# Four of the eight output jobs of the last block move behind its projections, and a staging tile gets a second place

## The chip, the cores and the metric

The kernel runs on one core of a Trainium2 chip. The metric is the device time of one execution in microseconds (us); of a set of timed executions the median counts. Engines: PE (TensorE, matmuls), DVE (VectorE), ACT (ScalarE), POOL (GpSimd) and SP (SyncE, which issues nearly all DMAs here). Each engine runs its own instructions strictly in the order in which they were written for it, and waits on semaphores for the others.

## The reference, cut to what matters

Two residual layers on x of shape (1, 2048, 1024). Layer 0 is RWKV-7 time mixing beside a gated short convolution, layer 1 a Conformer convolution beside a Mamba-2 SSD. The change lies in layer 1:

```python
p = h @ od_w_in[j]                      # 2048 x 1024 times 1024 x 3080
y_c = conformer_conv_mix(p[..., :CF_COLS], cf_conv_w[j], cf_conv_b[j], cf_ln_g[j], cf_ln_b[j])
y_d = mamba2_ssd_mix(p[..., CF_COLS:], ...)
y = jnp.concatenate([y_c, y_d], axis=-1) @ od_w_out[j]     # 2048 x 1024 times 1024 x 1024
x = x + gate[:, None, :] * rms_norm(y, norm_post[i])

def conformer_conv_mix(p, conv_w, conv_b, ln_g, ln_b):
    val, glu_gate, g = jnp.split(p, 3, axis=-1)
    u = val * jax.nn.sigmoid(glu_gate)
    u = causal_dwconv(u, conv_w) + conv_b                  # 31 taps
    u = jax.nn.silu(layer_norm(u, ln_g, ln_b))             # over 512 channels
    return u * jax.nn.silu(g)
```

## The kernel before

The 2048 rows are worked in four blocks of 512 (`NB` = 4). A block of layer 1 is a list of 25 projection jobs (`odd`): `dt`, eight tiles for the SSD's x, B and C (`evac_xbc`), four SSD gates, then four groups of three for the Conformer (GLU gate, value, gate). A job is 24 matmuls of 128x512 (8 parts of the contraction, each in three products of split fp32) into one of three PSUM tiles `pp`; only `dt` has 16. After the value job of group g, `evac_val` writes `u`, and `conv31` runs 30 multiply-adds `co<-u,cfw,co` on DVE. When the last gate is out, `conf_out` (lines 1281 to 1325) transposes the four `co` tiles by PE, takes mean and variance (`bst`, `bmv`), normalises to `xn`, transposes back, and for each of the four groups writes a tile `cs` with ACT, multiplies twice on DVE, splits it (`yh` by ACT, the rest by DVE) and stores both to DRAM (`y<-yh`, `y<-cs`). `cs` comes from `take`, which waits, while the order is being written, until the former holder has been freed; it is freed when its store is issued.

An output job multiplies one tile of 128 rows of y with one half (`dh`) of the output weights. It loads its y by two DMAs `w<-y` of 512 KB; the weights of a half are loaded into one of two large tiles (`act0`, `act1`) by eight DMAs `act<-wo` of 512 KB. The other large tile holds the block's h. Each row tile has two output jobs. The first to run only keeps its product: ACT squares and copies it to `yo`, which goes to DRAM (`od<-yo`). The second finishes the tile: it loads the row tile `x` (512 KB, two places) and the kept half (`yo<-od`), then ACT squares, DVE adds up (`ss`), POOL takes the root, DVE does `pp<-pp,ss,gp`, `x<-x,pp` and `yo<-yo,ss,gp`, POOL adds `x<-x,yo`, and SP stores the row tile (`out<-x`).

Three things set the order. `tile_trunk` makes one list of jobs by hand: `put(block, at, what)` places something behind the projection number `at` of a block, and what is added to a block's list comes behind its last projection. `run_jobs` writes the jobs in that order, and after every fourth matmul (`pace`) `tick` lets one step of each queue of side work follow (convolution, SSD chunks, evacuations, stores). `Feed.fetch` loads the operands of up to two jobs ahead; for an output job it first waits until all eight y tiles of that block have had their stores issued (`when=ready(t)`). All row tiles of the last block are therefore out of reach until `conf_out` of that block is through.

In the last block eight output jobs stand among the projections: half 0 of row tiles 4 to 7 behind projections 3, 5, 7 and 9, half 1 of the same behind 12, 13, 15 and 16. Behind the last projection come half 1 and then half 0 of tiles 8 to 11, and then tiles 12 to 15 (the last block's own) in pairs of both halves, eight jobs. The weights are loaded three times: half 0, half 1, and half 0 again.

Of the kernel before, what the change touches and what calls it, by code (L numbers as in the profile page):

```python
# [18 lines left out]
P = 128  # L19
# [3 lines left out]
BL = 512  # L23
# [125 lines left out]
class Trunk:  # L149
# [1134 lines left out]
    def conf_out(self, b, st):  # L1284
        nc = self.nc
        V, A, G, TE = nc.vector, nc.scalar, nc.gpsimd, nc.tensor
        add, mult = ALU.add, ALU.mult
        t = self.t
        co, cg = st["co"], st["cg"]
        xn = []  # L1290
        yield from self.pause(8)
        for q in range(4):
            ps = yield from self.take("tr", [P, BL], 2)
            for g in range(4):
                TE.transpose(out=ps[:, g * P:(g + 1) * P], in_=co[g][:, q * P:(q + 1) * P], identity=self.ident)
            yield
            sts = self.small.tile([P, 6], F32, name="bst")
            V.bn_stats(out=sts, in_=ps)
            mv = self.small.tile([P, 2], F32, name="bmv")
            V.bn_aggr(out=mv, in_=sts)  # L1300
            G.tensor_scalar(out=mv[:, 1:2], in0=mv[:, 1:2], scalar1=1e-5, scalar2=None, op0=add)
            G.tensor_tensor(out=mv[:, 1:2], in0=mv[:, 1:2], in1=self.nhalf[:, 0:1], op=ALU.pow)
            yield from self.pause(3)
            x = t.tile([P, BL], F32, name="xn", bufs=4)
            V.tensor_scalar(out=x, in0=ps, scalar1=mv[:, 0:1], scalar2=mv[:, 1:2], op0=ALU.subtract, op1=mult)
            self.free(ps)
            xn.append(x)
            yield
        for g in range(4):
            ps = yield from self.take("tr", [P, BL], 2)  # L1310
            for q in range(4):
                TE.transpose(out=ps[:, q * P:(q + 1) * P], in_=xn[q][:, g * P:(g + 1) * P], identity=self.ident)
            yield
            w = yield from self.take("cs", [P, BL])
            A.activation(out=w, in_=ps, func=AF.Identity, scale=self.col("cf_g", g, g + 1), bias=self.col("cf_lb", g, g + 1))
            th = t.tile([P, BL], F32, name="pr", bufs=2)
            A.activation(out=th, in_=ps, func=AF.Tanh, scale=self.hcfg[:, g:g + 1], bias=self.hcflb[:, g:g + 1])
            self.free(ps)
            yield
            V.scalar_tensor_tensor(out=w, in0=th, scalar=1.0, in1=w, op0=add, op1=mult)  # L1320
            V.scalar_tensor_tensor(out=w, in0=w, scalar=0.25, in1=cg[g], op0=mult, op1=mult)
            self.free(cg[g])
            yield from self.y_store(1, b, g, w)
            yield
# [229 lines left out]
def tile_trunk(ctx, tc, I, out, T):  # L1554
    k = Trunk(ctx, tc, I, out, T)
    k.setup()
    NB = T // BL
    with ExitStack() as e:
        k.st = e.enter_context(tc.tile_pool(name="st0", bufs=1))
        k.t = e.enter_context(tc.tile_pool(name="t0", bufs=1))  # L1560
        k.even_setup()
        blocks = [k.even(b) for b in range(NB)]
        list(k.first_block([o[0] for o in blocks[0][:BEGUN]]))
        blocks[0] = blocks[0][BEGUN:]
        k.slow += [k.modulation(0, range(16, 24), 1), k.modulation(1, range(24), 1), k.gate_row(0)]
        keys = iter(range(4 * NB))

        def outs(l, ts, dh):
            key = "wo", next(keys)
            return (lambda: k.urgent.append(k.w_out(l, dh, key))), k.out_jobs(l, ts, dh, key)  # L1570

        ahead = lambda l, b, spread=1: [lambda: k.urgent.append(k.hblock(l, b, spread))]

        def put(block, at, what):

            n = [i for i, o in enumerate(block) if not callable(o) and o[2][0] != "wo"][at - 1] + 1 if at else 0
            while n < len(block) and (callable(block[n]) or block[n][2][0] == "wo"):
                n += 1
            block[n:n] = what

        split_wo = lambda l: [(I["w_out"][l, dh][:, k2 * D:(k2 + 1) * D], k.wo[l][dh][2 * k2:2 * k2 + 2]) for dh in range(2) for k2 in range(KT // 2)]
        split_w = [(I["w_in1"][j], k.w1[j]) for j in range(24)] + [(I["w_in1"][24], k.wdt)]
        put(blocks[1], 0, [lambda: k.slow.append(k.presplit(split_wo(0) + split_w + split_wo(1)))])
        for b in range(NB - 1):
            put(blocks[b], AHEAD0, ahead(0, b + 1))
        load, jobs = zip(*[outs(0, range(8), dh) for dh in range(2)])
        at = 1, 4, 5, 7, 8, 10, 11, 13, 14, 14, 19, 21, 23, 25
        for p, o in zip(at, [load[0], *jobs[0], load[1], *jobs[1][:4]]):
            put(blocks[-1], p, [o])
        put(blocks[-1], 32, ahead(1, 0, 2))  # L1590
        blocks[-1] += jobs[1][4:]
        order = sum(blocks, [])
        blocks = [k.odd(b) for b in range(NB)]
        tiles = lambda b: range(4 * b, 4 * b + 4)
        at = 1, 3, 5, 7, 9, 9, 12, 13, 15, 16
        for b, (l, ts) in enumerate([(0, tiles(2)), (0, tiles(3)), (1, tiles(0)), (1, tiles(1))]):
            last = b == NB - 1
            load, jobs = zip(*[outs(l, ts if not dh or not last else range(4, 4 * NB), dh) for dh in range(2)])
            for p, o in zip(at, [load[0], *jobs[0], load[1], *jobs[1][:4]]):
                put(blocks[b], p, [o])  # L1600
            if not last:
                put(blocks[b], at[-1], ahead(1, b + 1, 2))
            if b == 1:
                put(blocks[1], 23, [lambda: k.slow.append(k.gate_row(1))])
        again, first = outs(1, range(8, 4 * NB), 0)
        blocks[-1] += [again, *jobs[1][4:8], *first[:4]] + [j for two in zip(jobs[1][8:], first[4:]) for j in two]
        order1 = sum(blocks, [])
        feed = Feed(k, order + order1)
        k.run_jobs(order, feed)
        k.drain(k.ev, k.quick, k.aux, k.urgent, k.bg, k.post, k.tail)  # L1610
    with ExitStack() as e:
        k.st = e.enter_context(tc.tile_pool(name="st1", bufs=1))
        k.t = e.enter_context(tc.tile_pool(name="t1", bufs=1))
        k.odd_setup()
        k.gated, k.pace = False, PACE[1]
        k.run_jobs(order1, feed)
        k.drain(k.ev, k.quick, k.aux, k.bg, k.post, k.tail)
    return k
# [47 lines left out]
```

## Time and profile before

| | us |
|---|---|
| median of three runs | 2455.23 |
| lowest and highest | 2452.19, 2456.57 |
| the profiled execution | 2446.16 |
| its span, first to last instruction | 2444.4 |
| PE busy in it | 2208.9 (90%) |
| DVE busy in it | 1753.1 (72%) |
| mean granted TensorE clock | 0.947 of full speed |

The page gives each engine's share over the whole span; over 40 slices PE is busy nine tenths or more in most, and five and seven tenths in the last two. Where time can be won or lost is read from the stretch around the last block, from about 2095 us, by the time lines of PE, DVE, ACT and POOL, and from the chain of waits that ends last. In a time line a bracket at the end of a row gives the idle time of that engine ahead of it and what ended it.

### The profile page before, as it was taken

How to read it: one execution, taken by the hardware profiler on the slowest of the kernel's cores; microseconds unless marked ns; L12 is line 12 of the kernel's file. 1: busy time of each engine (PE TensorE's matmuls, PEld its weight loads, DVE VectorE, ACT ScalarE, POOL GpSimd, SP SyncE). 2: the span in 40 equal slices, each digit the busy share in tenths (PEclk: the TensorE clock that was granted, in tenths of full speed). 3: DMA queues.
4: the chain of work that ended last, by engine and by line, in shares of the span. 5: the costliest groups of instructions: out<-in, count | busy, mean ns of one | idle time of the engine just before them, and what ended most of it. 6: DMA issues, size and time to landing. Idle time of an engine off the chain costs nothing. (4 is left out here: it accounts for less than half of the span.)

```text
span 2444.4 us, 36532 instructions
## 1 busy us (share of the span) xinstructions
PE 2208.9 (90%) x13408; PEld 1728.7 (71%) x13408; DVE 1753.1 (72%) x3340; ACT 811.4 (33%) x1731; POOL 593.3 (24%) x792
## 2 busy tenths in 40 slices
PE   6688889898988989989999979999999999999957
PEld 4566667676766767667777667877778787878836
DVE  6797897867857778565377443689589859967961
ACT  4334223433233322221222432353443525252221
POOL 2544535335253140221042310210020012002021
PEclk9788989999898999999999989999999999999978
DMA  8675676776776544544788678867877786787756
GB/s 302 223 254 179 216 260 226 234 251 226 248 237 215 199 122 159 190 129 139 254 292 268 235 266 296 301 226 254 293 252 248 243 298 207 267 275 276 244 178 232
DMA packets 232390, 575.18 MB, mean 235 GB/s; under 512 B 20498, under 2 KB 70418, under 8 KB 232212
## 3 DMA queue, kind: packets, MB, share of 16 engines
q1 hardware_dynamic: 232068, 572.59, 69.2%
q8 instruction: 106, 1.74, 0.3%
q14 instruction: 72, 0.59, 0.1%
q10 hardware_dynamic: 144, 0.26, 0.0%
HBM read 436.91 MB, written 135.86 MB: 234 GB/s over the span
## 5 line engine op out<-in xcount | busy, mean ns | idle before, releaser
L111 PE MATMUL pp<-act,w 128*128 128x512 f32 x7000 | 1797.8, 408 | 47.0 <-DMA w<-y 22.0
L111 PEld LDWEIGHTS pp<-act,w 128*128 128x128 f32 x7000 | 1312.5, 193 | 343.5 <-DMA w<-y 22.4
L111 DVE SCALAR_TENSOR_TENSOR co<-u,cfw,co 128x512 f32<-128x512 f32 x480 | 345.3, 754 | 6.1 <-ACT co L111 5.8
L111 POOL TENSOR_SCALAR ss<-ss 128x1 f32<-128x1 f32 x80 | 27.0, 338 | 639.5 <-DVE ss L111 463.2
L111 POOL TENSOR_TENSOR x<-x 128x512 fp32r<-128x512 f32 x80 | 109.0, 1376 | 134.8 <-ACT x L111 134.2
L111 POOL TENSOR_SCALAR sp<-S,PL 128x64 f32<-128x64 f32 x128 | 66.2, 531 | 194.1 <-DVE S L111 193.8
L111 DVE TENSOR_TENSOR pr<-X,BK 128x2 f32<-128x2 f32 (+30 forms) x248 | 101.6, 410 | 6.2
L111 ACT ACTIVATE tA<-pp 128x512 f32<-128x512 f32 x64 | 38.1, 596 | 203.4 <-PE pp L111 201.5
L111 POOL TENSOR_TENSOR w<-x,w 128x512 fp32r<-128x512 f32 x57 | 83.6, 1479 | 56.6 <-ACT w L111 56.4
L111 DVE TENSOR_REDUCE X<-pr 128x1 f32<-128x2 f32 (+30 forms) x248 | 86.5, 349 | 6.1
L111 ACT ACTIVATE q<-pp,cp 128x512 f32<-128x512 f32 x65 | 44.7, 688 | 128.6 <-PE pp L111 106.8
L111 DVE TENSOR_TENSOR UV<-ch,scal 64x128 f32<-64x128 f32 x128 | 36.9, 289 | 58.3 <-PE ch L111 56.3
L111 POOL COPY q<-carry 128x1 f32<-128x1 f32 (+1 forms) x84 | 38.6, 460 | 155.0 <-DVE tG L111 65.0
L111 POOL COPY carry<-q 128x1 f32<-128x1 f32 (+1 forms) x84 | 22.3, 265 | 221.8 <-ACT q L111 172.3
L111 POOL TENSOR_TENSOR x<-x,yo 128x512 f32<-128x512 f32 x32 | 48.5, 1516 | 104.0 <-DVE yo L111 91.5
L111 DVE TENSOR_TENSOR ss<-oss 128x1 f32<-128x1 f32 x32 | 6.0, 189 | 92.1 <-ACT tA L111 92.0
L111 ACT CAST x<-x 128x512 fp32r<-128x512 f32 x80 | 46.6, 616 | 72.6 <-DMA w<-w 19.5
L111 DVE SCALAR_TENSOR_TENSOR tG<-pp,derived,q 128x512 f32<-128x512 f32 x65 | 48.4, 744 | 30.9 <-ACT q L111 30.5
L111 DVE TENSOR_TENSOR act<-tr,act 128x256 fp32r<-128x256 f32 (+1 forms) x120 | 51.3, 436 | 24.1 <-ACT act L111 23.4
L111 PE MATMUL tr<-cc,h 128*128 128x128 f32 x224 | 39.6, 293 | 31.8 <-ACT h L111 28.6
L111 DVE STREAM_TRANSPOSE BK<-SC 32x1024 f32<-32x1024 f32 x32 | 63.8, 1993 | 0.5
L111 ACT ACTIVATE yo<-pp 128x512 f32<-128x512 f32 x32 | 19.1, 597 | 127.9 <-PE pp L111 112.6
(273 smaller groups left out, 3164.6 us busy)
## 6 DMA issues: line engine op xcount, KB each, us to landing
w<-w SPq DMA_DIRECT2D x450, 512.0 KB, 4.3
w<-y SPq DMA_DIRECT2D x128, 512.0 KB, 4.4
act<-wo SPq DMA_DIRECT2D x88, 512.0 KB, 6.1
x<-in_w_in_dram SPq DMA_DIRECT2D x58, 512.0 KB, 5.5
w<-x SPq DMA_DIRECT2D x96, 256.0 KB, 3.4
h<-in_ada_w_dram SPq DMA_DIRECT2D x32, 512.0 KB, 4.9
y<-yh SPq DMA_DIRECT2D x64, 256.0 KB, 3.1
wo<-x SPq DMA_DIRECT2D x64, 256.0 KB, 3.5
```

What stands on the lines that cost most here:

```text
L111: return f(*args, **kw)
```

## The change

`cs` gets two places, so that group g+1 may be written while group g is still on its way to DRAM; this holds for all four blocks of layer 1. And the last block's order changes: only half 0 of row tiles 4 to 7 stands among the projections, behind 5, 10, 15 and 18. Behind the last projection stand half 0 of tiles 8 to 11, half 1 of tiles 4 to 11, and the eight jobs of tiles 12 to 15 in pairs: twelve jobs ahead of those eight, where there were eight. The weights are loaded twice, half 0 and then half 1.

```diff
-            w = yield from self.take("cs", [P, BL])
+            w = yield from self.take("cs", [P, BL], 2)
...
-        for b, (l, ts) in enumerate([(0, tiles(2)), (0, tiles(3)), (1, tiles(0)), (1, tiles(1))]):
-            last = b == NB - 1
-            load, jobs = zip(*[outs(l, ts if not dh or not last else range(4, 4 * NB), dh) for dh in range(2)])
-            for p, o in zip(at, [load[0], *jobs[0], load[1], *jobs[1][:4]]):
+        for b, (l, ts) in enumerate([(0, tiles(2)), (0, tiles(3)), (1, tiles(0))]):
+            load, jobs = zip(*[outs(l, ts, dh) for dh in range(2)])
+            for p, o in zip(at, [load[0], *jobs[0], load[1], *jobs[1]]):
                 put(blocks[b], p, [o])
...
-        again, first = outs(1, range(8, 4 * NB), 0)
-        blocks[-1] += [again, *jobs[1][4:8], *first[:4]] + [j for two in zip(jobs[1][8:], first[4:]) for j in two]
+        load, jobs = zip(*[outs(1, range(4, 4 * NB), dh) for dh in range(2)])
+        for p, o in zip((1, 5, 10, 15, 18), [load[0], *jobs[0][:4]]):
+            put(blocks[-1], p, [o])
+        blocks[-1] += [load[1], *jobs[0][4:8], *jobs[1][:8]] + [j for two in zip(jobs[0][8:], jobs[1][8:]) for j in two]
```

PE at the start of the last block, before: `pp_19145` is projection 3, `pp_19230` (on `act0`) the first output job, `pp_19288` projection 4. The matmuls of the two are interleaved where the output job's weights are still arriving.

```order
L111 MATMUL pp_19145<-act1_62,w_19066 128x512 x12
L111 MATMUL tr_19171<-cc_88,tA_19097 128x16 x4
L111 MATMUL pp_19145<-act1_62,w_19068 128x512 x12
L111 MATMUL pp_19230<-act0_61,w_19100 128x512 x12
L111 MATMUL pp_19230<-act0_61,w_19102 128x512 x6
L111 MATMUL pp_19288<-act1_62,w_19146 128x512 x7
L111 MATMUL pp_19230<-act0_61,w_19102 128x512 x3
L111 MATMUL pp_19288<-act1_62,w_19146 128x512 x4
L111 MATMUL pp_19230<-act0_61,w_19102 128x512 x3
L111 MATMUL pp_19288<-act1_62,w_19146 128x512
L111 MATMUL pp_19288<-act1_62,w_19148 128x512 x12
```

After: projections 4 (`pp_19230`) and 5 (`pp_19277`) follow at once, then an output job (`pp_19332`) and projection 6 (`pp_19395`).

```order
L111 MATMUL pp_19145<-act1_62,w_19066 128x512 x12
L111 MATMUL tr_19171<-cc_88,tA_19097 128x16 x4
L111 MATMUL pp_19145<-act1_62,w_19068 128x512 x12
L111 MATMUL pp_19230<-act1_62,w_19100 128x512 x12
L111 MATMUL pp_19230<-act1_62,w_19102 128x512 x12
L111 MATMUL pp_19277<-act1_62,w_19146 128x512 x12
L111 MATMUL pp_19277<-act1_62,w_19148 128x512 x12
L111 MATMUL pp_19332<-act0_61,w_19231 128x512 x12
L111 MATMUL pp_19332<-act0_61,w_19233 128x512 x12
L111 MATMUL pp_19395<-act1_62,w_19278 128x512 x12
```

So the first output job stands two projections later. Of the later ones, projection 15 (the first value job) has two output jobs ahead of it in the block in place of six.

PE at the end, before: the back transposes of the last two groups (`tr<-cc,xn`), and behind them the first job of tile 12, `pp_21343`.

```order
L111 MATMUL tr_21305<-cc_88,xn_21155 128x128
L111 MATMUL tr_21305<-cc_88,xn_21191 128x128
L111 MATMUL tr_21305<-cc_88,xn_21240 128x128
L111 MATMUL tr_21305<-cc_88,xn_21272 128x128
L111 MATMUL tr_21321<-cc_88,xn_21155 128x128
L111 MATMUL tr_21321<-cc_88,xn_21191 128x128
L111 MATMUL tr_21321<-cc_88,xn_21240 128x128
L111 MATMUL tr_21321<-cc_88,xn_21272 128x128
L111 MATMUL pp_21343<-act0_61,w_21339 128x512 x12
L111 MATMUL pp_21343<-act0_61,w_21341 128x512 x12
```

After: the last group's transposes (`tr_21232`) stand within the cover job `pp_21225`, a whole further one (`pp_21281`) follows, and then the first job of tile 12, `pp_21329`.

```order
L111 MATMUL pp_21225<-act1_62,w_21094 128x512 x4
L111 MATMUL tr_21232<-cc_88,xn_20942 128x128
L111 MATMUL tr_21232<-cc_88,xn_20994 128x128
L111 MATMUL tr_21232<-cc_88,xn_21045 128x128
L111 MATMUL tr_21232<-cc_88,xn_21081 128x128
L111 MATMUL pp_21225<-act1_62,w_21094 128x512 x8
L111 MATMUL pp_21225<-act1_62,w_21096 128x512 x12
L111 MATMUL pp_21281<-act1_62,w_21166 128x512 x12
L111 MATMUL pp_21281<-act1_62,w_21168 128x512 x12
L111 MATMUL pp_21329<-act0_61,w_21325 128x512 x12
```

All sixteen back transposes had no matmul between them; now they lie among the last four of the cover jobs that stand ahead of tile 12.

DVE at the same place, before: groups 2 and 3 of `cs`, and then the first finishing step of tile 12 (`ss_21428`).

```order
L111 SCALAR_TENSOR_TENSOR cs_21312<-pr_21314,cs_21312 128x512
L111 SCALAR_TENSOR_TENSOR cs_21312<-cs_21312,cg_20754 128x512
L111 TENSOR_TENSOR cs_21312<-cs_21312,yh_21318 128x512
L111 SCALAR_TENSOR_TENSOR cs_21328<-pr_21330,cs_21328 128x512
L111 SCALAR_TENSOR_TENSOR cs_21328<-cs_21328,cg_20879 128x512
L111 TENSOR_TENSOR cs_21328<-cs_21328,yh_21334 128x512
L111 TENSOR_TENSOR ss_21428<-oss_167 128x1
```

After: the last instruction on `cs_21245`, which the last store waits for, stands behind `ss_21321` and `pp_21281`, the finishing steps of the last cover job.

```order
L111 TENSOR_TENSOR x_21215<-x_21215,pp_21165 128x512
L111 SCALAR_TENSOR_TENSOR cs_21202<-cs_21202,cg_20566 128x512
L111 TENSOR_TENSOR cs_21202<-cs_21202,yh_21212 128x512
L111 SCALAR_TENSOR_TENSOR cs_21245<-pr_21247,cs_21245 128x512
L111 SCALAR_TENSOR_TENSOR yo_21274<-yo_21274,ss_21277,gp_17033 128x512
L111 SCALAR_TENSOR_TENSOR cs_21245<-cs_21245,cg_20700 128x512
L111 TENSOR_TENSOR ss_21321<-oss_167 128x1
L111 SCALAR_TENSOR_TENSOR pp_21281<-pp_21281,ss_21321,gp_17033 128x512
L111 TENSOR_TENSOR cs_21245<-cs_21245,yh_21255 128x512
L111 TENSOR_TENSOR x_21271<-x_21271,pp_21225 128x512
```

So finishing steps of cover jobs now lie between the steps of the last groups, and the last of them ahead of the last store.

## Rows read from the trace of the kernel before

**Rows 1.** Chain that ended last: start us, us, what.
```profile
2382.91 0.70 DVE cs L111
...
2383.62 2.47 DMA y<-cs
...
2386.37 3.66 DMA w<-y
...
2390.07 45.97 PE pp L111 x192
...
2436.07 0.60 ACT tA L111
...
2437.31 0.55 POOL ss L111
```

**Rows 2.** Time line of PE, 2300 to 2445 us: start, length, engine, operation, count, [idle].
```profile
2299.72 32.81 PE L111 MATMUL pp<-act,w 128*128 128x512 f32 x144
...
2344.26 0.44 PE L111 MATMUL tr<-cc,co 128*128 128x128 f32 x2 [2.38 <-DVE co L111]
...
2366.97 1.11 PE L111 MATMUL tr<-cc,xn 128*128 128x128 f32 x4 [6.33 <-ACT pr L111]
2390.07 45.96 PE L111 MATMUL pp<-act,w 128*128 128x512 f32 x192 [21.98 <-DMA w<-y]
```

**Rows 3.** Time line of DVE, 2105 to 2400 us, same columns.
```profile
2200.65 0.16 DVE L111 TENSOR_TENSOR ss<-oss 128x1 f32<-128x1 f32 x1 [9.07 <-ACT tA L111]
...
2220.14 0.69 DVE L111 SCALAR_TENSOR_TENSOR u<-tA,pp 128x512 f32<-128x512 f32 x1 [2.90 <-PE pp L111]
...
2231.95 0.76 DVE L111 SCALAR_TENSOR_TENSOR pp<-pp,ss,gp 128x512 f32<-128x512 f32 x1 [0.72 <-POOL ss L111]
...
2234.53 0.74 DVE L111 SCALAR_TENSOR_TENSOR yo<-yo,ss,gp 128x512 f32<-128x512 f32 x1
...
2236.46 1.78 DVE L111 SCALAR_TENSOR_TENSOR co<-u,cfw,co 128x512 f32<-128x512 f32 x1
...
2343.47 0.74 DVE L111 SCALAR_TENSOR_TENSOR co<-u,cfw,co 128x512 f32<-128x512 f32 x1
```

**Rows 4.** Time line of ACT, 2095 to 2225 us.
```profile
2104.80 0.59 ACT L111 COPY u<-pp 128x512 f32<-128x512 f32 x1 [4.53 <-PE pp L111]
...
2122.04 0.57 ACT L111 COPY u<-pp 128x512 f32<-128x512 f32 x1
...
2131.28 0.57 ACT L111 COPY u<-pp 128x512 f32<-128x512 f32 x1
```

**Rows 5.** Time line of PE, 2060 to 2300 us.
```profile
2110.88 25.01 PE L111 MATMUL pp<-act,w 128*128 128x512 f32 x109 [0.46 <-DMA act<-wo]
...
2226.14 0.60 PE L111 MATMUL tr<-cc,sz 128*128 128x128 f32 x4
...
2262.47 0.66 PE L111 MATMUL tr<-cc,sy 128*128 128x128 f32 x4 [2.10 <-ACT sy L111]
```

**Rows 6.** Time line of POOL, 2195 to 2265 us.
```profile
2203.25 1.28 POOL L111 TENSOR_TENSOR x<-x,yo 128x512 f32<-128x512 f32 x1 [1.52 <-DVE yo L111]
...
2235.36 2.34 POOL L111 TENSOR_TENSOR x<-x,yo 128x512 f32<-128x512 f32 x1 [2.65 <-DVE yo L111]
```

**Rows 7.** DMA issues, 2320 to 2360 us: count, KB each, median us to landing.
```profile
w<-y SPq DMA_DIRECT2D x4, 512.0 KB, 5.3
out_dram<-x SPq DMA_DIRECT2D x4, 512.0 KB, 2.7
x<-x SPq DMA_DIRECT2D x3, 512.0 KB, 3.3
```

**Rows 8.** Busy time by stretch: engines' busy us (instructions), granted clock, DMA share, GB/s.
```profile
2300.00:2320.00 20.00, 20.00 (x90) 16.58 (x89) 20.00 (x32) 4.29 (x11) 0.00 (x0) 1.00 0.96 341
```

**Rows 9.** The same by 5 us, around the start of the last eight jobs.
```profile
2385.00:2390.00 5.00, 0.00 (x0) 0.00 (x0) 0.00 (x0) 0.00 (x0) 0.00 (x0) 0.50 0.66 197
2390.00:2395.00 5.00, 4.93 (x12) 3.91 (x13) 0.00 (x0) 0.00 (x0) 0.00 (x0) 0.53 1.03 419
```

**Rows 10.** Waits of PE in the blocks before, 1560 to 2105 us: total, times, longest.
```profile
PE tr L111 <- ACT pr L111: 2.5, 3, 1.1
```

More of the change, by code (lines that the diff above doesn't have):

```diff
@@ L1595, in tile_trunk @@
         at = 1, 3, 5, 7, 9, 9, 12, 13, 15, 16
-        for b, (l, ts) in enumerate([(0, tiles(2)), (0, tiles(3)), (1, tiles(0)), (1, tiles(1))]):
-            last = b == NB - 1
-            load, jobs = zip(*[outs(l, ts if not dh or not last else range(4, 4 * NB), dh) for dh in range(2)])
-            for p, o in zip(at, [load[0], *jobs[0], load[1], *jobs[1][:4]]):
+        for b, (l, ts) in enumerate([(0, tiles(2)), (0, tiles(3)), (1, tiles(0))]):
+            load, jobs = zip(*[outs(l, ts, dh) for dh in range(2)])
+            for p, o in zip(at, [load[0], *jobs[0], load[1], *jobs[1]]):
                 put(blocks[b], p, [o])
-            if not last:
-                put(blocks[b], at[-1], ahead(1, b + 1, 2))
+            put(blocks[b], at[-1], ahead(1, b + 1, 2))
             if b == 1:
                 put(blocks[1], 23, [lambda: k.slow.append(k.gate_row(1))])
-        again, first = outs(1, range(8, 4 * NB), 0)
-        blocks[-1] += [again, *jobs[1][4:8], *first[:4]] + [j for two in zip(jobs[1][8:], first[4:]) for j in two]
+        load, jobs = zip(*[outs(1, range(4, 4 * NB), dh) for dh in range(2)])
+        for p, o in zip((1, 5, 10, 15, 18), [load[0], *jobs[0][:4]]):
+            put(blocks[-1], p, [o])
+        blocks[-1] += [load[1], *jobs[0][4:8], *jobs[1][:8]] + [j for two in zip(jobs[0][8:], jobs[1][8:]) for j in two]
         order1 = sum(blocks, [])
```

## Prediction

> **What bounds the kernel now.** Times are those of the profiled execution; a count of instructions is read from the order of the code, a duration from a row. I read the chain of waits that ended last, from its end [rows 1]. It ends with 46 us in which PE works through the last eight jobs without a pause, and a tail of 8.4 us. What stands ahead is no work of PE: multiply on `cs`, store, load of `w`, and only then the first of the eight. The time line of PE shows what that costs [rows 2]. From 2299.7 on PE has covering jobs; at 2341.88 (2344.26 less 2.38) it begins to wait for the last `co`; until 2390.07 it waits again and again, 6.33 us once with ACT's `pr` named (the single place of `cs`), at the last 21.98 us for `w<-y`. All its waits there come to some 37 us (2.38, 0.77, 3.25, 1.79, 0.68, 6.33, 21.98; the two ends and the largest are in the rows). That is what the change can take away at most.
>
> When does the last `co` come? The time line of DVE [rows 3]: idle by 9.07 us ahead of 2200.65, `u` of the first group at 2220.14, and from there nearly without a gap to the last `co`, 2343.47 plus 0.67. So two distances set the end: when the first value job is done, and 124.0 us of DVE.
>
> **The change part by part.** *1. The first value job comes earlier.* One job is 24 matmuls at 32.81/144 = 0.228 us [rows 2], 5.47 us. Two output jobs stand ahead of projection 15 in place of six: 4 x 5.47 = 21.9 us.
>
> Not all of it arrives. After, projections 4 to 7 come with fewer jobs between them, and ACT is not faster for that. ACT copies `u` out of the PSUM tile at 2104.80, 2122.04 and 2131.28 [rows 4]. Three jobs behind the first PE would want that tile at 2104.8 + 3 x 5.47 = 2121.2; it is free at 2122.6 (wait 1.4). The next is wanted at 2128.1 and free at 2131.85 (wait 3.8). Together 5.2; some of it before waits as well, 0.46 at 2110.88 [rows 5]. I take 4. Below, the copies may themselves move up, since they follow DVE, which has slack there: 0. Above, if ACT and DVE keep their whole old pace: 9. `u` of the first group then comes at 2220.1 - 21.9 + 4 = 2202.2.
>
> *2. DVE to the last `co`.* Three of the four finishing jobs leave this stretch. Each takes `pp` 0.76, `yo` 0.74, a wait for POOL's root 0.72, `x` (as long as `yo`, estimate), and a collision: while POOL adds, a `co` lasts 1.78 in place of 0.74, and that add 2.34, where one with DVE at rest lasts 1.28 [rows 3, 6]. 3.8 us a job without overlaps, 11.4 for three. Three small SSD steps come in, of at most 0.74, together 1.6: 124.0 - 11.4 + 1.6 = 114.2, the last `co` at 2316.4. The other value jobs don't hold it up: one follows every three to four jobs (16 to 22 us), and a group takes DVE 28.5.
>
> The Trainium skill says of this collision (SBUF — State Buffer, Who interferes with whom) that a DVE instruction with two SBUF inputs contends with a GpSimd instruction that reads SBUF; the trace agrees, 1.78 against 0.74. By that rule the three collisions, some 3 us, go for good, and others come up behind the last `co`, where DVE has slack.
>
> *3. PE to the transposes of the last `co`.* Before, from 2220.1 to 2341.88: 121.7 us for 19 jobs, the SSD, and one wait of 2.10 at 2262.47 [rows 5]. After: 18 jobs, 116.2, so 2318.4. Both sides meet within 2 us: PE's wait for `co` goes, and from here PE sets the time. What was at 2344.26 is now at 2318.4, 25.9 us earlier. Below, PE waits up to 6 us for DVE; above, nothing more, since PE's own work stays.
>
> *4. From there to the last eight jobs.* Before 45.8 us. After, PE has 142 matmuls of covering jobs (32.4 us) and 24 transposes, 0.60 for four [rows 5], 3.6; with 1 us for the steps of the normalisation, the last covering job ends at 2355.4. `cs` with two places and the covering jobs thus hide the 6.33 and its neighbours. But a new chain stays open: the last multiply on `cs` stands on DVE behind `ss` and `pp` of the last covering job, so it waits for that job's square and root. Each has a row at the end of the program: PE's end 2436.04 to root 2437.86, 1.8; then `pp` 0.76, `cs` 0.70, store with issue 2.75, load of `w` 3.70 [rows 1, 3], and on SP two loads (`x`, `yo`) issued between store and load, some 0.7. Together 10.4 us in place of 21.98. Start of the last eight: 2365.8, 24.3 earlier than 2390.07. Bounds: 8 if SP runs ahead, 16 if the store queues behind a stored row tile (2.7) and a loaded one (3.3) [rows 7].
>
> *5. The load on the DMAs.* Eight finishing jobs in a row, before four. Each moves y 1 MB, `od` 0.25, `x` 0.5, `out` 0.5, in binary units 2.36 MB, in some 6 us: 390 GB/s. While y and weights were loaded at once, the DMA share was 0.96 at 341 GB/s [rows 8]; in 5 us around 2392 it was 419 [rows 9]. At 341 a job takes 6.9 us; the y of the first jobs is loaded well ahead, up to four jobs by SP's order, and hides the most. I take 1.3, bounds 0 and 8. The eight weight loads that go lie in the stretch of the projections, where PE hardly waits for DMAs: 0 to -0.5.
>
> The Trainium skill speaks against the change here: DMA: Bandwidth & Descriptors, Specifications, gives about 358 GB/s of memory bandwidth for a core. By it the eight jobs' 18.9 MB would take 52.8 us, an estimate, against some 49 at PE's pace, which would cost 3 to 4 us; the 419 over 5 us lies above that figure, the 341 below it, so the trace doesn't settle it.
>
> *6. The rest.* The last eight jobs stay at 46.0 and the tail at 8.4. PE restarted before at a granted clock of 0.53, after 0.50 in the pause [rows 9]; a shorter pause may give 0 to 2 back, I take 0. In the three blocks before, `cs` with two places can take at most the 2.5 us that PE waits for `pr` in 1560 to 2105 [rows 10]; the next job of each block covers `conf_out` there, so 0, bounds -2 and 2 for moved DVE work.
>
> **Sum:** 24.3 - 1.3 = 23 us. Span 2444.4 - 23 = 2421.4, profiled 2423; the median lies 9 us above the profiled execution, and 2455.2 - 23 = **2432**.
>
> **The rivals.** *A: The DMAs set the pace of the finishing jobs.* For it: 0.96 at 341 GB/s. Against: the y that is loaded ahead, and the 419. With 6.9 us a job in place of 5.9 the last covering job ends 7 us later: gain 16, 2439; with 8 us a job gain 9. So 2438 to 2448.
>
> *B: More than I count.* ACT moves up (0 in place of 4 in part 1), the chain in part 4 takes 8, the clock gives 2 back: gain 30 to 36, 2419 to 2425.
>
> *C: Slower, by the two places of `x`.* A tile's `out` waits for POOL's add, the load of the next `x` into that place for `out`, and on SP the further y loads, and at last the stores of `y`, stand behind both. If in effect only one tile is in flight, a job costs 6 (square to add, an estimate from the steps in part 2 and the root) + 2.7 + 3.3 [rows 7] = 12 us. The first finishing job ends near 2312.5; seven more give 2396 in place of 2355, so the end comes 16 us later than before: 2471. It decides from 9.6 us a job. Against it: two places give two jobs for the 12 us, and SP has the y of three finishing jobs issued ahead of the first such wait.
>
> *D: Nothing moves.* What the projections gain they lose again in the stretch of part 1, because ACT and DVE were its true pace and PE waits for them: `u` of the first group would come at about 2218, and the eight fewer weight loads and the new order would weigh up. 2450 to 2458. Against: DVE is idle by 9 us ahead of 2200, the work there isn't full.
>
> **How the numbers follow.** The forecast of 2432 (2425 to 2438, gain 17 to 30) 0.62; A 0.20; B 0.07; D 0.05; C 0.06. The range takes the forecast, nearly all of B and three quarters of A: 2420 to 2445, leaving out about 0.18. About 0.2%, 5 us, is what a measurement can tell: faster by more holds the forecast, A and B, 0.89; within it D, 0.05; slower C, 0.06.
>
> **What would show it.** In the profile after: `u` of the first group near 2202 and PE waits of some 4 us behind projections 4 to 7 (part 1); the last `co` near 2316 without a `co` of 1.78 beside it more than once or twice (part 2); no wait of PE for `co` above 6 us (part 3); PE busy until near 2355, then one wait of about 10 us named `w<-y` (part 4); finishing jobs about 6 us apart (part 5). I am wrong if PE waits for `x`, `y` or weights between 2310 and 2355 (A, C), if the single wait ahead of the last eight jobs is 20 us again, or if `u` of the first group is hardly earlier (D).

## The result, and the profile after

The changed kernel took 2427.62 us in the median of four executions (2423.76 to 2428.93), the kernel before 2454.56: a ratio of 0.9888, 95% interval 0.9871 to 0.9905. Run again beside other kernels it stood at 2434.06 and a ratio of 0.9915 (0.9897 to 0.9932). By these ratios it is faster by 27 us (23 to 32) and by 21 us (17 to 25); 2432 was forecast.

The profiled execution of the changed kernel has a span of 2427.1 us, that of before 2444.4, only 17.3 more. The medians differ by 9.6 us more; the start of the last block accounts for 5.7 of these, and of the rest, which lies between the profiled and the other executions, there is no trace. Each block of layer 1 begins with the same two waits of ACT for PE; the copy `u<-pp` behind the first of them is a landmark in every trace. Its line in ACT's time line of before (start, length, engine, operation, and in brackets the idle time ahead and what ended it):

```profile
2098.74 0.58 ACT L111 COPY u<-pp 128x512 f32<-128x512 f32 x1 [4.86 <-PE pp L111]
```

And in that of after:

```profile
2104.44 0.59 ACT L111 COPY u<-pp 128x512 f32<-128x512 f32 x1 [4.86 <-PE pp L111]
```

The last block began 5.7 us later here. Over the fourteen profiled executions of this study its start lies between 2098.74 and 2113.68, and most of that spread (1429.5 to 1445.4) is there at the first `u<-pp` of layer 1, before any code that differs. The shown execution of before is the earliest of all. The blocks ahead of the last show no gain from the second place of `cs` clear of their scatter: from the first `u<-pp` of layer 1 to the landmark the two executions of before took 669.3 and 669.2 us, the two of after 671.6 and 669.8, all others 666.7 to 673.6. Distances from the landmark repeat: to the first matmul of the last eight jobs 291.33 and 291.67 us in two executions of before, 268.19 and 268.20 in two of after. **The stretch became 23.1 us shorter**; this is the size that the prediction is held against below.

Two names are used below: covering jobs are the output jobs between the last projection and the last eight, and finishing jobs are those among them that finish a row tile. The chain that ended last, after, from the last covering jobs (start, length, what; "issue" is time in which the engine waited for nothing that the profile shows), beside [rows 1]:

```profile
2358.25 0.61 DVE cs L111
2359.13 0.28 issue
2359.41 0.78 ACT pr L111
2360.22 0.69 DVE cs L111
2360.91 0.66 DVE yo L111
2361.57 0.60 DVE cs L111
2362.60 0.56 POOL ss L111
2363.22 0.63 issue
2363.85 1.71 DVE cs L111
2365.58 2.80 DMA y<-cs
2368.45 4.04 DMA w<-y
```

PE's time line of the same stretch, beside [rows 2]:

```profile
2319.76 0.44 PE L111 MATMUL tr<-cc,co 128*128 128x128 f32 x2 [0.39 <-DVE co L111]
...
2324.78 0.63 PE L111 MATMUL tr<-cc,co 128*128 128x128 f32 x4 [1.37 <-DVE bmv L111]
...
2336.23 0.33 PE L111 MATMUL tr<-cc,xn 128*128 128x128 f32 x1 [1.81 <-DVE xn L111]
...
2348.70 10.27 PE L111 MATMUL pp<-act,w 128*128 128x512 f32 x44
2372.63 46.12 PE L111 MATMUL pp<-act,w 128*128 128x512 f32 x192 [13.66 <-DMA w<-y]
```

Of PE's seven waits of 37.2 us four are left, 17.2 us: the last covering job ends at 2358.97, and then one wait of 13.66 us stands where 21.98 was. DVE, beside [rows 3]:

```profile
2204.07 0.68 DVE L111 SCALAR_TENSOR_TENSOR u<-tA,pp 128x512 f32<-128x512 f32 x1
...
2317.38 2.32 DVE L111 SCALAR_TENSOR_TENSOR co<-u,cfw,co 128x512 f32<-128x512 f32 x3
```

`u` of the first group comes 99.6 us behind the landmark (before 121.4), the last `co` ends at 2319.70, 115.6 us behind `u` (before 124.0).

### The profile page after: what moved, and what is told of

It reads as the page before. It is cut to its first block, busy times and chain, and to the rows that moved or that the text cites. A ratio compares the mean times of both kernels' runs of the same rounds, so it can differ in the third digit from the quotient of the medians.

```text
span 2427.1 us, 36527 instructions
## 1 busy us (share of the span) xinstructions
PE 2212.8 (91%) x13408; PEld 1733.3 (71%) x13408; DVE 1753.9 (72%) x3340; ACT 811.9 (33%) x1731; POOL 593.2 (24%) x792
## 4 chain that ended last, share of the span: by engine, by line
PE 53%; DVE 25%; DMA 8%; POOL 5%; ACT 5%; issue 4%; SPq 0%; POOLq 0%; DVEq 0%; ACTq 0%
PE pp L111 40%; PE tr L111 6%; PE ch L111 3%; PE yp L111 3%; DVE BK L111 2%; DVE pr L111 2%; DVE co L111 2%; DVE X L111 2%; POOL ss L111 2%; DVE SC L111 1%; DVE scal L111 1%; DMA w<-x 1%; DVE h L111 1%; DVE yo L111 1%; DVE AR L111 1%
## 5 line engine op out<-in xcount | busy, mean ns | idle before, releaser
L111 PE MATMUL pp<-act,w 128*128 128x512 f32 x7000 | 1805.6, 409 | 39.0 <-DMA w<-y 13.7
L111 PEld LDWEIGHTS tr<-cc,h 128*128 128x128 f32 x224 | 29.1, 151 | 45.5 <-ACT h L111 37.3
```

What stands on the lines that cost most here:

```text
L111: return f(*args, **kw)
```

## The experiments

Every kernel was profiled. Since the start of the last block moves by up to 15 us from execution to execution, the comparison goes by distances from the landmark; the timed ratios against before, with their intervals, stand beside them.

| kernel | landmark | to first `u` | to the last eight jobs | PE's wait ahead of them | to the span's end | ratio of times to before |
|---|---|---|---|---|---|---|
| before | 2098.74 | 121.4 | 291.33 | 21.98 | 345.7 | 1 |
| before, again | 2105.13 | 121.5 | 291.67 | 22.00 | 345.8 | |
| order alone | 2105.58 | 100.9 | 283.56 | 27.72 | 337.5 | 0.998 (0.9959 to 1.0) |
| two places alone | 2101.47 | 120.7 | 281.10 | 16.91 | 335.9 | 0.9944 (0.9926 to 0.9961) |
| **after** | 2104.44 | 99.6 | 268.19 | 13.66 | 322.7 | 0.9888 (0.9871 to 0.9905) |
| after, again | 2112.28 | 99.7 | 268.20 | 13.65 | 322.3 | 0.9915 (0.9897 to 0.9932) |
| after, jobs at 3, 5, 7, 9 | 2110.75 | 109.6 | 272.07 | 18.23 | 326.8 | 0.9915 (0.9894 to 0.9937) |
| after, three among | 2105.64 | 94.1 | 261.46 | 9.01 | 316.1 | 0.9865 (0.9842 to 0.9888) |
| after, two among (15, 18) | 2104.49 | 97.0 | 261.64 | 2.58 | 319.5 | 0.9895 (0.9865 to 0.9926) |
| after, stores placed earlier | 2101.05 | 99.8 | 268.24 | 13.50 | 322.2 | 0.9906 (0.9877 to 0.9934) |
| after, three places | 2101.48 | 99.7 | 264.20 | 9.62 | 318.4 | 0.9881 (0.9853 to 0.9909) |
| after, rows not stored | 2113.68 | 99.5 | 263.71 | 6.78 | 317.5 | one execution |
| three among, three places | 2109.12 | 94.0 | 263.27 | 9.33 | 319.2 | 0.9877 (0.9854 to 0.99) |
| two among (5, 18), three places | 2109.58 | 94.1 | 255.91 | 4.77 | 314.8 | 0.9863 (0.9841 to 0.9885) |

**The two halves of the change, each alone.** First the order without the second place:

```diff
-            w = yield from self.take("cs", [P, BL], 2)
+            w = yield from self.take("cs", [P, BL])
```

> The changed order, but the staging tile cs with one place as before. Theory 1 (both halves of the change are needed): with one place each group of cs waits until the store of the one ahead has been issued, so the groups come about 7 to 9 us apart, as before (y<-cs at 2362.3, 2369.8, 2376.7, 2383.6), and the last two fall behind the last covering job: the wait ahead of the last eight jobs grows from 13.7 to some 18 to 22 us, and the gain over the kernel before falls to 16 to 22 us. Rival (the covering jobs hide the single place): within 3 us of the whole change, 24 to 30 us faster than before.

Only 7.8 us came of it, less than half of what either side allowed at its low end. The last `co` came 1.3 us later than in the whole change, as `u` did, but PE's wait ahead of the last eight jobs grew to 27.72 us. ACT's time line shows why:

```profile
2355.59 0.60 ACT L111 ACTIVATE tA<-pp 128x512 f32<-128x512 f32 x1 [5.25 <-PE pp L111]
2356.18 0.77 ACT L111 ACTIVATE cs<-tr,cp 128x512 f32<-128x512 f32 x1
...
2368.91 0.78 ACT L111 ACTIVATE cs<-tr,cp 128x512 f32<-128x512 f32 x1 [6.54 <-DMA y<-cs]
...
2378.32 0.78 ACT L111 ACTIVATE cs<-tr,cp 128x512 f32<-128x512 f32 x1 [4.42 <-DMA y<-cs]
```

Groups 2 and 3 wait for the store of the group ahead; group 1 has no such wait, but stands in ACT's order behind the squares `tA` of three covering jobs, and starts 17.1 us after group 0. So the direction of theory 1 held and its size was too small: with covering jobs between the groups a single place costs more than the 7 us that a group took in the kernel before.

> The kernel before, with two places of cs and nothing else. Theory 1 (the single place is a price of its own): groups 1 and 3 follow their forerunner by 2 to 3 us in place of 7, so the last store comes 8 to 10 us earlier, and with it the end: 6 to 12 us faster than before. Rival (the chain from the last co through the normalisation sets the end, not the place): within 2 us of before.

Two places in the kernel before (the same line, the other way round) gave 10.2 us, within the range. The 6.33 us of [rows 2] went to 0.22, and the stores came in pairs. SP's time line:

```profile
2366.02 0.37 SPq L111 DMA_DIRECT2D y<-cs  x1
2367.99 0.41 SPq L111 DMA_DIRECT2D y<-cs  x1
2374.06 0.36 SPq L111 DMA_DIRECT2D y<-cs  x1
2376.08 0.36 SPq L111 DMA_DIRECT2D y<-cs  x1
```

By time this version stands at 0.9944 of before and the new order alone at 0.998, whose interval reaches 1.0. By distance, 7.8 and 10.2 make 18.0; together they gave 23.1. Each is worth more with the other: the second place 15.4 us in the new order, the new order 12.9 us with two places.

**Where the date of the first value job counts.** Four output jobs ahead of it in place of two:

```diff
-        for p, o in zip((1, 5, 10, 15, 18), [load[0], *jobs[0][:4]]):
+        for p, o in zip((1, 3, 5, 7, 9), [load[0], *jobs[0][:4]]):
```

> The whole change, but the four output jobs stand behind projections 3, 5, 7 and 9 in place of 5, 10, 15 and 18, so four stand ahead of the first value job and not two. Theory 1 (the date of the first value job sets the end): u of the first group comes 10.9 us later, so do the last co and the start of the last eight jobs less what DVE can make up; 6 to 11 us slower than the whole change. Rival (PE's number of jobs sets the end, which is the same here): within 2 us of the whole change.

`u` came 10.0 us later, the last `co` 13.6, the last eight jobs only 3.9: between the two. The covering jobs take up most of it, since PE works through them at the same dates (the last ends 253.8 us behind the landmark, after 254.5), and only the wait behind them grows, from 13.7 to 18.2. So a later value job is paid for only as far as it makes the last store of `y` later.

One output job fewer among the projections:

```diff
-        for p, o in zip((1, 5, 10, 15, 18), [load[0], *jobs[0][:4]]):
+        for p, o in zip((1, 5, 15, 18), [load[0], *jobs[0][:3]]):
...
-        blocks[-1] += [load[1], *jobs[0][4:8], *jobs[1][:8]] + [j for two in zip(jobs[0][8:], jobs[1][8:]) for j in two]
+        blocks[-1] += [load[1], *jobs[0][3:8], *jobs[1][:8]] + [j for two in zip(jobs[0][8:], jobs[1][8:]) for j in two]
```

> The whole change carried on: three output jobs among the projections (behind 5, 15 and 18) and thirteen covering jobs behind. Theory 1 (the last y store follows the last co, PE's work up to the last covering job stays the same): u of the first group 5.5 us earlier, the wait of 13.7 us ahead of the last eight jobs falls to 8 to 10, 3 to 6 us faster than the whole change. Rival (the steps of the last cs groups are tied to the covering jobs by DVE's and ACT's order, as the last multiply on cs standing behind pp of the last covering job): the wait stays at 12 to 14 us, and the time within 2 us of the whole change.

Theory 1 held: `u` 5.5 us earlier, the wait at 9.01, the last eight jobs 6.7 us earlier (3 to 6 were expected). But more changed than the date. The last multiply on `cs` (2358.15 in DVE's time line) now stands ahead of `pp` of the last covering job (2361.10) and no longer behind it, and the chain that ends PE's wait runs through transfers: the store of a row tile, 9.05 us, the load of the next `x`, 2.70, then `pp` of the last but one covering job, the multiply, the store of `y` and the load of `w`.

The same with `(1, 15, 18)` and two jobs:

> Two output jobs among the projections (behind 15 and 18) and fourteen covering jobs behind; none stands ahead of the first value job. Theory 1 (the first value job's date sets when the last y is stored, PE's count of covering jobs the rest): u of the first group 5.5 us earlier than with three, the wait ahead of the last eight jobs falls from 9.0 to 4 to 6 us, the start of the last eight, counted from the same copy at the start of the block, 3 to 5 us earlier than with three (261.5). Rival (with no job between projections 1 to 15, ACT and DVE set the pace there): u of the first group gains 0 to 2 us and the end the same 0 to 2.

Here both fell by their numbers, though the rows bear out the rival's reason. The wait did shrink, to 2.58, but the last eight jobs start no earlier than with three, and `u` comes 2.9 us later. PE's waits from 2120 to 2205 us:

```profile
2128.41 5.74 PE L111 MATMUL pp<-act,w 128*128 128x512 f32 x24 [1.59 <-ACT u L111]
2136.55 5.99 PE L111 MATMUL pp<-act,w 128*128 128x512 f32 x18 [2.40 <-ACT u L111]
...
2150.65 0.93 PE L111 MATMUL tr<-cc,sx 128*128 128x128 f32 x4 [3.40 <-DVE xn L111]
```

With no job between projections 1 and 15, PE waits there for 9.2 us in place of 4.6. And behind the waits the granted clock fell: in slices of 2 us it was 0.80 and 0.50 (the lower of the clock's two levels, 1.2 of 2.4 GHz) from 2136 to 2140, behind the waits of 1.59 and 2.40, 1.00 again from 2142 on, and 0.71 and 0.50 from 2150 to 2154, behind the wait of 3.40. Busy time by stretch (PE busy, granted clock, DMA share, GB/s):

```profile
2124.00:2134.00 10.00, 8.41 (x37) 1.00 0.50 161
2134.00:2144.00 10.00, 7.60 (x31) 0.83 0.33 110
2144.00:2154.00 10.00, 5.96 (x27) 0.84 0.50 159
```

With three jobs it was 1.00 in the same stretches. 4.6 us more waits and up to 3 us of slower clock (0.17 and 0.16 of 10 us each, an estimate) outweigh the 5.5 us of the job that left. At the end of this version the chain runs over stores of row tiles (7.42, 6.32 and 6.08 us, from 2361.38 on), and the span ends 3.4 us later behind the landmark than with three jobs.

**What holds the last store of `y`.** Two edits for one question:

```diff
-        self.later(STORE, store)
+        self.later(2 if l else STORE, store)
```

> The whole change, but in layer 1 the stores of y are placed 2 steps (8 matmuls) behind their multiply in the program and not 8 steps (32 matmuls). Theory 2 (groups 2 and 3 of cs wait for a place, and a place comes free only when the store is issued, which the fixed delay puts 7.3 us of PE later): the last store comes 4 to 6 us earlier, the wait ahead of the last eight jobs falls from 13.7 to 8 to 10 us, the distance from the start of the block to the last eight from 268.2 to 262 to 265. Rival (the last groups are held by DVE's and ACT's steps for the covering jobs): 267 to 269.

Nothing came of it at the end: 268.24 us. Group 2 kept its date (250.0 us behind the landmark, 249.8 after), behind the squares of the same three covering jobs, so the fixed delay is not what holds it. Group 3 lost its wait for a store, and the last store of `y` was issued 1.3 us earlier (259.9 against 261.1), but took 4.06 us in the chain in place of 2.80.

```diff
-            w = yield from self.take("cs", [P, BL], 2)
+            w = yield from self.take("cs", [P, BL], 3)
```

> The whole change with three places of cs. Theory 2 (the groups wait for a place): group 2 no longer waits, group 3 waits for group 0 alone; last store 3 to 6 us earlier, the distance from the start of the block to the last eight 262 to 266 in place of 268.2. Rival (held by DVE's and ACT's steps for the covering jobs): 267 to 269.

A third place gave 4.0 us. ACT's time line of after:

```profile
2353.62 0.60 ACT L111 ACTIVATE tA<-pp 128x512 f32<-128x512 f32 x1 [5.25 <-PE pp L111]
...
2354.21 0.77 ACT L111 ACTIVATE cs<-tr,cp 128x512 f32<-128x512 f32 x1
...
2356.61 0.78 ACT L111 ACTIVATE cs<-tr,cp 128x512 f32<-128x512 f32 x1 [0.96 <-DMA y<-cs]
```

And with three places:

```profile
2340.13 0.78 ACT L111 ACTIVATE cs<-tr,cp 128x512 f32<-128x512 f32 x1 [0.62 <-PE tr L111]
...
2350.72 0.60 ACT L111 ACTIVATE tA<-pp 128x512 f32<-128x512 f32 x1 [4.27 <-PE pp L111]
2351.30 0.77 ACT L111 ACTIVATE cs<-tr,cp 128x512 f32<-128x512 f32 x1
```

With two places, group 2 stands in ACT's order behind the squares of three covering jobs (2341.73, 2347.68 and 2353.62), and group 3 right behind it, after 0.96 us of wait for a store. With three, group 2 stands behind one square (2338.83) and group 3 behind two more (2344.79 and 2350.72). So the last multiply on `cs` (2356.63) came ahead of the last covering job's steps on DVE. The place decides, not the delay of the store; why the earlier placing of the stores left group 2 where it was stays open.

**Do the DMAs set the pace of the finishing jobs?**

```diff
             def store():
-                self.nc.sync.dma_start(out=self.x1[t] if l == 0 else self.out[t * P:(t + 1) * P], in_=x)
+                if l == 0 or not 4 <= t < 12:
+                    self.nc.sync.dma_start(out=self.x1[t] if l == 0 else self.out[t * P:(t + 1) * P], in_=x)
```

> The whole change, with the stores of row tiles 4 to 11 to out left out (those rows are not written, 4 MB less on the DMAs); a place of x is free again right after POOL's add. Rival A of the prediction (the DMAs or the two places of x set the pace of the eight finishing jobs): PE's waits between the transposes of co and the last covering job (some 3.6 us) go, the last covering job ends 3 to 6 us earlier. My theory (PE's own work sets that pace): it ends within 1.5 us of the whole change, 254.5 us from the start of the block, and only the wait ahead of the last eight jobs shrinks, by 1 to 3 us.

The last covering job ended 256.9 us behind the landmark, not earlier than 254.5, and PE's waits for DVE were still there, 1.37 for `bmv` and 2.90 for `xn`. So nothing here says that the stores set the pace of the finishing jobs. (Behind the wait of 2.90 the granted clock was 0.55 and 0.59 for 4 us: the twelve matmuls there took 4.39 us in place of 3.03, and the wait was 1.1 longer, which makes up the 2.4 us.) The wait ahead of the last eight jobs fell to 6.78 us, much more than I had expected. But the edit changed more than the transfers: groups 2 and 3 now stand behind one covering job's square each, and on DVE the last multiply on `cs` stands ahead of the last covering job's `pp` and not behind it:

```profile
2369.29 0.68 DVE L111 TENSOR_TENSOR cs<-cs,yh 128x512 fp32r<-128x512 f32 x1
...
2373.54 0.76 DVE L111 SCALAR_TENSOR_TENSOR pp<-pp,ss,gp 128x512 f32<-128x512 f32 x1 [0.95 <-POOL ss L111]
```

The last store of `y` was issued at 2370.00, ahead of the end of the last covering job at 2370.61. How much of the 6.9 us is that order, and how much the transfers, this run does not tell. In the whole change a store of a row tile took 4.3 us (median of issues in 2320 to 2360 us), before 2.7 [rows 7].

**Carried on, and the next bound.**

> The changed kernel once more, beside the two versions carried on. From the start of the last block to the last eight jobs it takes 268 us again; the start of the block itself may lie anywhere between 2098 and 2114 us, as it did in ten executions, so single times differ by some 10 us. 23 to 30 us faster than before.

268.20 us, as in the first execution; the ratio was 0.9915, which is 21 us (17 to 25), a little under the 23 to 30 expected.

> Three output jobs among the projections and three places of cs together. Each alone shortened the distance from the start of the block to the last eight jobs, 268.2, to 261.5 and 264.2. Theory 1 and 2 together (the date of the first value job and the places are separate prices): 256 to 259, the wait of PE ahead of the last eight 4 to 7 us, 8 to 12 us faster than the changed kernel. Rival (the next bound is the chain of x and out on the DMAs, as with two jobs among the projections): 260 to 262 or a wait for x within the last jobs, within 1 us of three jobs among the projections alone.

The rival's reason held: 263.27, nothing gained over three jobs alone (261.46), rather some 2 us lost. The last covering job ended 253.9 us behind the landmark (252.5 with three jobs alone; behind a wait of 1.98 us twelve matmuls took 4.57 us here in place of 3.00), and the chain that ends the wait is transfers alone:

```profile
2351.01 8.11 DMA out_dram<-x
2359.18 1.38 DMA x<-x
2360.56 5.86 DMA y<-cs
2366.55 5.71 DMA w<-y
```

> Two output jobs among the projections, behind 5 and 18 (so that one still stands between the first projections), and three places of cs. Theory 1 with the reason for the miss of two jobs behind 15 and 18 (there the stretch of projections 1 to 8 had no job to cover ACT and DVE): u of the first group within 1 us of three jobs (94.1 us from the start of the block). The end: PE's own work sets it, or the chain of x and out, which the version behind 15 and 18 showed with 7 us for one store; the last eight start at 254 to 260, and the time lies within 4 us of three jobs with three places.

With a job back behind projection 5, `u` is at 94.1 and the slow stretch is gone: the reason given for the two-job version holds. The wait of 4.77 us ahead of the last eight jobs is here one for DVE's `pp` and not for `w<-y`. The last eight jobs start at 255.91, 12.3 us earlier than after, but 4.4 us of that are lost again behind them; the end is 7.8 us nearer (314.8 against 322.7). Part of its chain that ended last:

```profile
2360.86 7.60 DMA out_dram<-x
...
2369.39 6.28 DMA out_dram<-x
...
2376.65 7.25 DMA out_dram<-x
...
2385.32 7.64 DMA od<-yo
2393.03 3.76 DMA yo<-od
```

PE is no longer in it from 2360.86 on: stores of row tiles, stores and loads of kept halves, and SP's order set the end; which of the transfers' length, the two places of `x` and SP's order weighs most was not separated. On the same chip, in turn with it, this version took 2423.51 us against 2434.06 of the changed kernel, and the two ratios to before, 0.9863 (0.9841 to 0.9885) and 0.9915 (0.9897 to 0.9932), have no value in common: it beats both kernels (the changed kernel's first ratio, 0.9871 to 0.9905, does overlap). Three jobs with two places is as good by its ratio, 0.9865 on another chip, and needs no third place. Four places of `cs` were not tried.

> The kernel before once more. The distance from the start of the last block to the last eight jobs is 291 us again within 1 us, and the start of the block lies later than 2098.7, which was the earliest of ten executions; so the 9 us between the profiled execution and the median of before lie ahead of the last block.

Both parts held: 291.67, and a start of the block at 2105.13, 6.4 us later, in an execution that was 6.5 us longer.

One part of the change was not run alone: the third load of the weights, which goes. In the kernel before, PE's waits from 2100 to 2345 us name the weights once, with 0.46 us [rows 5].

## Why the prediction was right

The 23 us of the sum are the 23.1 us by which the stretch shrank, but two errors of some 4 us cancelled. Distances from the landmark, the prediction's converted with the 2098.74 of the execution that it argues from:

| | predicted | measured |
|---|---|---|
| `u` of the first group | 103.5 | 99.6 |
| end of the last `co` | 217.7 | 215.3 |
| PE at the transposes of the last `co` | 219.7 | 215.3 |
| end of the last covering job | 256.7 | 254.5 |
| start of the last eight jobs, with 1.3 for the DMAs | 268.4 | 268.2 |

**Part 1.** The 21.9 us were right (21.8 came), the 4 us taken off were not. PE's waits from the landmark to `u`, in total, times, longest, after:

```profile
PE tr L111 <- DVE xn L111: 3.1, 4, 1.8
PE pp L111 <- ACT yo L111: 1.4, 1, 1.4
```

That is 4.5 us against 3.0 before, so 1.5 lost. A wait of 1.40 us came, the size computed for the copy `u`, but it is one for `yo`, the copy of the output job between the projections. PE's row, and two of ACT's:

```profile
2128.18 13.00 PE L111 MATMUL pp<-act,w 128*128 128x512 f32 x56 [1.40 <-ACT yo L111]
```

```profile
2127.54 0.59 ACT L111 COPY yo<-pp 128x512 f32<-128x512 f32 x1
...
2128.55 0.58 ACT L111 COPY u<-pp 128x512 f32<-128x512 f32 x1
```

The equal size is luck. PE went on when `yo` was out, 0.37 us before `u` was even begun, so it took the PSUM tile of the output job while the other two still held their projections, and each projection's tile was wanted a job later than the prediction had it. By that the wait of 3.8 did not come, and besides, ACT's third copy came 7.6 us behind the second and not 9.2. That ACT might move up was named as the lower bound. Another 1.4 us on the good side were not traced.

**Part 2.** 114.2 predicted, 115.6 measured; no `co` of 1.78 is left beside these steps. (The durations listed for a finishing job add up to 4.0 us, 0.2 more than the 3.8 that the sum uses.)

**Part 3.** The two sides did meet: 0.39 us of wait for `co`, and none of PE's waits from there to the last covering job named `x`, `y` or weights.

**Part 4** is the mis-sized one. From the transposes of the last `co` to the last eight jobs 48.7 us were predicted with the DMAs' 1.3, and 52.9 measured. PE waited 3.2 us for the normalisation, not 1 (`bmv`, `xn` in the rows above). And the chain behind the last covering job was of the kind described, the last multiply on `cs` behind `pp` of that job, but 13.7 us long and not 10.4; that lies within the bounds of 8 and 16, of which the upper had another reason, a store queued behind transfers. The excess: ACT began the square 1.1 us late (2360.08 against 2358.97), being busy with `pr` of group 3; `ss` stood 1.3 us behind on DVE, after the other steps on `cs` and `yo`; and the last multiply took 1.70 us in place of 0.70, because POOL's add ran beside it. ACT's time line, DVE's and POOL's have

```profile
2360.08 0.59 ACT L111 ACTIVATE tA<-pp 128x512 f32<-128x512 f32 x1
```

```profile
2363.85 1.70 DVE L111 TENSOR_TENSOR cs<-cs,yh 128x512 fp32r<-128x512 f32 x1
```

```profile
2363.74 1.26 POOL L111 TENSOR_TENSOR x<-x,yo 128x512 f32<-128x512 f32 x1 [0.59 <-DMA x<-x]
```

The step that failed is thus the sum of durations along one chain, which left out that the engines on it still had other work queued. (The other execution of after shows the same collision, 1.48 us; with the stores placed earlier the add came after the multiply, and it took 0.68.) The Trainium skill's rule on this collision (SBUF — State Buffer, Who interferes with whom) had been read as harmless behind the last `co`; here it fell on the one chain that was open, and cost 1.0 us.

What the prediction did not separate is the worth of the two halves. It had the second place "hide the 6.33 and its neighbours"; the runs show that without it the new order gives 7.8 us in all.

**Part 5.** The finishing jobs ran 6.6 us apart (2313.1 to 2358.97 for seven), where the sum had 6.1. The version without the stores kept DVE's waits and was no faster there, so no share of that was shown to be the DMAs'. What they cost in the wait behind, which part 5 did not count, is shown only for the versions carried on, where stores of row tiles stand in the chain.

The Trainium skill's 358 GB/s (DMA: Bandwidth & Descriptors, Specifications) is not borne out as a ceiling over 5 us here either. Busy time of a stretch in the version with two jobs and three places, the last two columns being DMA share and GB/s:

```profile
2381.00:2386.00 5.00, 4.47 (x21) 3.35 (x20) 0.76 (x1) 0.00 (x0) 1.50 (x2) 1.00 1.03 404
```

Over 20 us the changed kernel moved 348 from 2300 to 2320, at a share of 0.94, and 366 from 2290 to 2310, at 0.99.

**Part 6.** The last eight jobs took 46.1 us (46.0 forecast), the tail 8.4.

**The rivals.** A does not describe this change, but transfers are the next bound, as the versions with three and two jobs show; whether it is their length (A) or the two places of `x` (C) was not separated. C and D did not come: no row tile was held back to one at a time, and `u` was 21.8 us earlier. B came in one term, the whole date of the value job, and was eaten by part 4.

## What to carry to other kernels

Work that is moved behind a dependency helps in full only if the steps of the dependent chain are not queued behind that work on the other engines: count, for each step of the chain, what else stands ahead of it on its engine. A staging tile with one place between two engines and a store serialises the groups, and here it cost more, not less, when covering work was put between them: 15.4 us against 10.2. Where executions differ by more than the effect, a landmark that repeats in every trace gives distances that agree within a few tenths of a us.

## What the runs showed that was not expected

The start of the last block moved by 15 us between executions of programs that are the same up to layer 1, while the distances behind it repeated within 0.4 us. A store of 512 KB took 2.7 us (median) from 2320 to 2360 us before, at a DMA share of 0.68, 4.3 in the same stretch after, at 0.84, and 6.1 to 9.05 in the chains around the start of the last eight jobs in the versions with three or two jobs among the projections, at shares of 0.93 and more. And short waits of PE can cost more than their length: after waits of 1.59 and 2.40 us the granted clock fell to 0.50 in a slice of 2 us, after one of 3.40 again, and after one of 1.98 to 0.76 and then 0.50 for some 4 us, while waits of 1.37 and 1.81 in the changed kernel left it at 1.00. The length of the wait alone does not decide: one of 1.96 us, with three jobs among the projections, left it at 1.00 too.
